# Loads of the gate stage in one order, and each stage's first weights split ahead: a transformer block on one core

## The chip, the cores and the metric

The kernel runs on one core of a Trainium2 chip. The metric is the device time of one execution in microseconds. The core has engines that run side by side, each with its own list of instructions in a fixed order: TensorE (PE in the profile) multiplies matrices, VectorE (DVE) and ScalarE (ACT) work on tiles, GpSimd (POOL) does some of that and issues transfers, SyncE (SP) only issues transfers. An instruction waits for what it needs, and everything behind it on its engine waits with it.

## The reference

One encoder block on 512 tokens of width 2048, in fp32:

```
u   = RMSNorm_pre(h)
[q|k|v|conv_a|conv_b|gate_attn|gate_conv] = u @ W_in
y_A = NeighbourhoodAttention2D(q, k, v; bias) @ W_attn_o        # 8 heads of 128
y_B = ConformerConv(conv_a, conv_b) @ W_conv_o                  # GLU, conv 31, LayerNorm, swish
m   = sigmoid(gate_attn) * y_A + sigmoid(gate_conv) * y_B
h   = h + RMSNorm_post(m @ W_out)
h   = h + RMSNorm_post(SwiGLU(RMSNorm_pre(h)))                  # hidden width 5632
```

## The kernel before

**Products.** Tokens lie along the free axis, so a tile of activations is 128 channels x 512 tokens (a `slot`; u is un0 to un15, 16 tiles). Every fp32 operand is split in two fp32r parts, hi (a cast, on ACT) and lo (operand minus hi, on DVE), and a product is three matmuls: lo x hi, hi x hi, hi x lo. So ahead of each use of weights stand a load (SP's queue, into the pool tag `raw`, 5 buffers of 512 KB), a cast on ACT (names ending in h, or `whi_`) and a subtraction on DVE (`l`, `wlo_`).

**Strassen.** Most of the three large projections run as Winograd's form of Strassen on pairs of output blocks (`strassen`, line 233): seven products instead of eight. Weights come in quarters (tiles q), of which sums are made (s; s1 is made by a load and a second load that adds, `sums`). The activations' side (`operands`) is made once per stage: b11, b2 and the sums t12, t34 (`winograd_t`), each split (`merged`, lines 158 and 159). The products run in the order 11, T2, T1, T3 and so on; one is 8 matmuls with hi (line 265) and 8 with lo (line 267).

**Stages.** After convolution and attention comes the gate stage (lines 555 to 630): the first two of sixteen gate tiles are computed by plain products (tile g, lines 584 to 586), one chunk of u at a time over c = 0 to 7, and while these run, u is loaded back from DRAM (`u_d`), and the Strassen operands of the other tiles are made from it (b, t). The pairs g2, g3 and on follow. Then the gated outputs (`gated`) with the layer norm of the convolution's branch (`layer_norm`, called before tile LN_AT = 8), the output projection, and the FFN: five tiles plain, then pairs f5 to f43 on weights `w_gu`; the result of each pair goes to DRAM (`a_d`, scaled `as_d`). The down projection runs in two stages and a last part (`products_and_operands(n, ...)`, `pairs(n, ...)`, n = 0 and 1, then `half`): first a plain part over four chunks of the FFN (tiles fa, from loads ad; products pd, weights raw_w, whi_wd, wlo_wd, loaded by `weights`), during which the operands of the Strassen pairs are made from rows loaded as da (`prepare(c)`, c = 0 to 7; tiles dt and d), then eight pairs (d_0 to d_14). Results of the first stage are written to `y_d`, later ones added to it by transfers that POOL issues (yf from the plain part, ys from the pairs). The last part has four more chunks (fa40 to fa43, weights wl0 to wl15).

**Order.** A scheduler sets the order of each engine's list when the kernel is built, from program order and its own costs. Instructions marked with `keep_in_program_order` (`load_in_order` for loads) stay in the order in which they are written. Tiles come from pools in turn: a tile of a tag with 5 buffers waits until the tile five before it has been read for the last time. `early(k0)` loads the first three fa of a plain part ahead, `behind_last` splits them behind the last product of the stage before.

Of the kernel before, what the change touches and what calls it, by code (L numbers as in the profile page):

```python
# [25 lines left out]
F32 = mybir.dt.float32  # L26
# [5 lines left out]
P = 128  # L32
# [28 lines left out]
S1_AT = 3  # L61
# [9 lines left out]
def hybrid_block(ctx: ExitStack, tc, xT, vecs, rpb, mask, w_c0, w_qk, w_v, w_gg, w_cg, w_ao, w_co, w_out, w_g0, w_gu, w_dn, outT):  # L71
# [154 lines left out]
    def sums(w1, name):  # L226

        s1 = stp.tile([P, 1024], F32, tag="S1", name=f"{name}s1")
        nc.sync.dma_start(s1, w1[:, :1024])
        nc.gpsimd.dma_start(s1, w1[:, 1024:], accum_op=ALU.add)  # L230
        return s1

    def strassen(w0, w1, op, name, n, s1=None, behind_last=None):
# [8 lines left out]

        def quarter(w, c):
            raw = wp.tile([P, 1024], F32, tag="raw", name=f"{name}q", bufs=5)
            nc.sync.dma_start(raw, w[:, c * 1024 : (c + 1) * 1024])
            return raw
# [11 lines left out]
        def product(ps, w, b, first=False, last=False):  # L258
            hi = wp.tile([P, 1024], F32R, tag="whi", name=f"{name}h")
            nc.scalar.copy(hi, w)  # L260
            lo = wp.tile([P, 1024], F32R, tag="wlo", name=f"{name}l")
            nc.vector.tensor_tensor(out=lo, in0=w, in1=hi.bitcast(F32), op=ALU.subtract)
# [14 lines left out]
        a11, a21, a22, a12 = quarter(w0, 0), quarter(w1, 0), quarter(w1, 1), quarter(w0, 1)  # L277
        product(x, a11, "11", first=True)
# [57 lines left out]

    def rstd_row(acc, n, name):
        out = slot(f"{name}_bc")
        nc.scalar.copy(out, by_column(rstd(acc, n, name), name))
        return out  # L340
# [234 lines left out]
    raw, uf = [], []  # L575
    load_gate(0)
    load_un(0)
    for c in range(HT):
# [37 lines left out]
    for i in range(2, KT):  # L616
        c11, c12, c21, c22 = strassen(w_cg[2 * CT + i], w_cg[2 * CT + KT + i], op, f"g{i}", i + 1, s1 if i == 2 else None)
# [13 lines left out]
    def layer_norm():  # L631
        yc, cv = [], [slot(f"cr{i}") for i in range(CT)]
# [10 lines left out]
        rc = rstd_row(acc, CONV, "rc")  # L643
# [16 lines left out]
        return yc  # L660
# [10 lines left out]
    yg, m = [], []  # L671
    for i in range(KT):
        if i == LN_AT:
            yc = layer_norm()
# [94 lines left out]
    for c in range(HT):  # L769
        hi, lo = wchunk(w_g0[1, c], f"f1_{c}")  # L770
        for k in range(2):
# [64 lines left out]
    acts = []  # L836
    for j in range(5, FT):
        if j == FT - 2:
            behind = early(0)
        c11, c12, c21, c22 = strassen(  # L840
            w_gu[j], w_gu[FT + j], op, f"f{j}", j, behind_last=behind if j == FT - 1 else None
# [26 lines left out]
    def loaded(o, k0):  # L868

        raw = wraw(f"w{k0}_{o}")  # L870
        nc.sync.dma_start(
            raw.rearrange("p (n k) -> p n k", n=2), w_dn[o : o + 2, :, k0 * P : (k0 + DN_P) * P].rearrange("n p k -> p n k")
        )
        return raw

    def weights(o, k0):
        raw = loaded(o, k0)
        return wchunk(raw, f"wd{k0}_{o}", raw=raw)

# [13 lines left out]
    def products_and_operands(n, k0, add):  # L893
# [3 lines left out]
        def load_rows(c):  # L897
            rows.append([slot(f"da{c}_{i}") for i in range(2)])
            for i, t in enumerate(rows[c]):
                nc.gpsimd.dma_start(t, as_d[n * KT + c + i * HT])  # L900

        def prepare(c):
# [3 lines left out]
            u1, u2 = rows[c]  # L906
            b11.append(merged(u1[:, A], f"d11_{c}"))
            b2.append([merged(u2[:, cols], f"d2{c}_{i}") for i, cols in enumerate((A, B))])
            tt = stp.tile([P, 2, NT], F32, tag="S", name=f"dt{c}")
# [235 lines left out]
```

## Time and profile before

| | us |
|---|---|
| median of 3 runs (2541.95 to 2547.01) | 2544.56 |
| profiled execution | 2541.38 |
| its span | 2539.6 |
| PE busy in the span | 2499.8 (98%) |
| DVE busy | 2004.1 (79%) |
| ACT busy | 1194.1 (47%) |
| granted PE clock, mean | 0.995 |

The span runs from the first instruction to the last. A row of the timeline has the start and the duration of an instruction (or of several alike, xN), engine, line, operation, output and inputs, and in brackets the idle time of the engine ahead of it and what ended it. A row of the windows has the stretch in us from the span's start, its length, the busy time of PE, its weight loads, DVE, ACT and POOL with instruction counts, the granted clock, the share of the DMA engines' time and GB/s. A row of the waits names the engine and line that waited, what it waited for, and total, times and longest.

### The profile page before, as it was taken

To read this page: it belongs to the slowest core of one execution; us is meant where nothing else is said; L and a number is where in the kernel's file an instruction comes from. 1 tells how busy PE (TensorE), PEld (TensorE's weight loads), DVE (VectorE), ACT (ScalarE), POOL (GpSimd) and SP (SyncE) were. 2 spreads that over 40 slices of the span, in tenths; PEclk is the share of its full clock that TensorE was granted. 3 is DMA by queue.
4 is the path that set the end of the run, shared out by engine and by line. 5 is a ranking of instruction groups with operands and counts; after the bars stand their busy time and mean duration, and the time that the engine had idled before them with its cause. 6 is when DMAs were issued, how large, how long until landed. Compare 5 with 4: busy or idle time off the path is not lost.

```text
span 2539.6 us, 35631 instructions
## 1 busy us (share of the span) xinstructions
PE 2499.8 (98%) x13415; PEld 2158.5 (85%) x13415; DVE 2004.1 (79%) x2583; ACT 1194.1 (47%) x1822; POOL 477.4 (19%) x521
## 2 busy tenths in 40 slices
PE   9999999989999999999999999999999999999997
PEld 7888888878888888889988888888888888887887
DVE  5999896577776655338798888899998888879886
ACT  5223333355555422225455555555555565456453
POOL 0110222220000011001101111122222124442343
PEclk9999999999999999999999999999999999999998
DMA  6246332476667435327356665666666677889774
GB/s 211 90 146 203 104 101 101 148 246 197 184 183 243 167 126 193 100 99 209 112 157 169 180 180 172 178 202 205 202 199 202 208 255 218 242 218 222 182 223 151
DMA packets 153358, 452.42 MB, mean 178 GB/s; under 512 B 17889, under 2 KB 25185, under 8 KB 153185
## 3 DMA queue, kind: packets, MB, share of 16 engines
q1 hardware_dynamic: 100896, 320.12, 37.5%
q0 software_dynamic: 31616, 94.39, 17.3%
q10 hardware_dynamic: 20672, 35.63, 3.8%
q8 instruction: 105, 1.72, 0.3%
q14 instruction: 69, 0.56, 0.1%
HBM read 381.39 MB, written 61.87 MB: 175 GB/s over the span
## 4 chain that ended last, share of the span: by engine, by line
PE 85%; DVE 8%; issue 3%; DMA 2%; ACT 1%; POOL 1%; ACTq 0%; DVEq 0%; POOLq 0%; SPq 0%
PE f L265 20%; PE f L267 10%; PE d L265 8%; PE g L265 7%; PE d L267 4%; PE g L267 4%; PE qk L186 2%; PE qk L185 2%; PE qk L182 2%; PE po L185 2%; PE po L186 2%; PE po L182 2%; PE py L182 2%; PE py L186 2%; PE py L185 2%
## 5 line engine op out<-in xcount | busy, mean ns | idle before, releaser
L411 DVE SCALAR_TENSOR_TENSOR cv<-z,vec,cv 128x497 f32<-128x497 f32 (+14 forms) x240 | 190.7, 796 | 4.8
L136 DVE TENSOR_TENSOR wlo_wo<-raw_wo,whi_wo 128x1024 fp32r<-128x1024 f32 x36 | 47.4, 1318 | 106.6 <-ACT whi_wo L135 106.3
L801 POOL TENSOR_TENSOR row<-row,asq 128x512 f32<-128x512 f32 x30 | 41.1, 1370 | 413.9 <-ACT asq L800 413.9
L135 ACT CAST whi_wo<-raw_wo 128x1024 fp32r<-128x1024 f32 x36 | 37.9, 1054 | 130.0 <-PE po L185 122.7
L941 POOL TENSOR_TENSOR ys<-ys,row 128x512 f32<-128x512 f32 x32 | 55.7, 1742 | 130.6 <-DVE ys L303 85.4
L135 ACT CAST whi_y<-raw_y 128x1024 fp32r<-128x1024 f32 x32 | 33.5, 1052 | 79.4 <-PE py L185 76.2
L135 ACT CAST whi_qk<-raw_qk 128x1024 fp32r<-128x1024 f32 x32 | 33.7, 1052 | 77.1 <-PE qk L185 56.5
L136 DVE TENSOR_TENSOR wlo_qk<-raw_qk,whi_qk 128x1024 fp32r<-128x1024 f32 x32 | 40.1, 1254 | 32.6 <-ACT whi_qk L135 32.4
L668 DVE TENSOR_TENSOR gg<-py,gg 128x512 f32<-128x512 f32 x32 | 21.8, 689 | 52.7 <-PE py L186 52.7
L828 POOL TENSOR_TENSOR an<-an,row 128x512 f32<-128x512 f32 x32 | 50.7, 1584 | 67.5 <-DMA an<-a_d 42.4
L136 DVE TENSOR_TENSOR wlo_y<-raw_y,whi_y 128x1024 fp32r<-128x1024 f32 x32 | 53.3, 1667 | 10.9 <-ACT whi_y L135 10.0
L323 POOL TENSOR_TENSOR r_r<-r_v,mhalf 128x2 f32<-128x2 f32 (+1 forms) x6 | 7.0, 1171 | 265.8 <-DVE r_v L321 215.4
L182 PE MATMUL py<-ycl,whi_y 128*128 128x512 f32 x128 | 49.8, 389 | 0.0
L185 PE MATMUL py<-ych,whi_y 128*128 128x512 f32 x128 | 49.8, 389 | 0.0
L186 PE MATMUL py<-ych,wlo_y 128*128 128x512 f32 x128 | 49.8, 389 | 0.0
L861 ACT ACTIVATE sg<-sg 128x512 f32<-128x512 f32 x39 | 24.7, 634 | 50.2 <-DVE sg L303 50.2
L492 POOL TENSOR_TENSOR bm<-braw,msk 128x128 f32<-128x128 f32 x56 | 42.4, 791 | 14.8 <-DMA braw<-in_rpb 14.7
L678 POOL TENSOR_TENSOR gg<-gg,gg 128x512 f32<-128x512 f32 x16 | 20.6, 1288 | 112.2 <-ACT whi_y L135 70.7
L419 POOL TENSOR_TENSOR csum<-csum,cv 128x512 f32<-128x512 f32 x7 | 12.7, 1814 | 144.3 <-DVE cv L411 144.3
L164 PE MATMUL f<-b,whi_f 128*128 128x256 f32 x128 | 36.4, 285 | 0.7 <-DVE b L159 0.7
L166 PE MATMUL f<-b,wlo_f 128*128 128x256 f32 x128 | 36.2, 283 | 0.0
L165 PE MATMUL f<-b,whi_f 128*128 128x256 f32 x128 | 36.2, 283 | 0.0
(3196 smaller groups left out, 8752.5 us busy)
## 6 DMA issues: line engine op xcount, KB each, us to landing
raw_wo<-in_w_out SPq DMA_DIRECT2D x36, 512.0 KB, 3.8
raw_qk<-in_w_qk SPq DMA_DIRECT2D x32, 512.0 KB, 3.7
raw_w<-in_w_dn SPq DMA_DIRECT2D x24, 512.0 KB, 5.7
a_d<-sg ACTq DMA_DIRECT2D x44, 256.0 KB, 3.7
raw_v<-in_w_v SPq DMA_DIRECT2D x16, 512.0 KB, 4.3
raw_y<-in_w_ao SPq DMA_DIRECT2D x16, 512.0 KB, 3.8
gg<-g_d SPq DMA_DIRECT2D x32, 256.0 KB, 4.2
raw_y<-in_w_co SPq DMA_DIRECT2D x16, 512.0 KB, 3.6
```

The source lines that it names most:

```text
L135: cast(hi[:, s], raw[:, s])
L136: nc.vector.tensor_tensor(out=lo[:, s], in0=raw[:, s], in1=hi[:, s].bitcast(F32), op=ALU.subtract)
L182: mmul = nc.tensor.matmul(ps, hi[:, s], al, start=first, stop=False)
L185: nc.tensor.matmul(ps, hi[:, s], ah, start=False, stop=False)
L186: nc.tensor.matmul(ps, lo[:, s], ah, start=False, stop=last)
L265: nc.tensor.matmul(ps, hi[:, ws[k]], t, start=first and k == 0, stop=False, skip_group_check=True)
L267: nc.tensor.matmul(ps[:, A], lo[:, ws[k]], t[:, A], start=False, stop=last and k == HT - 1, skip_group_check=True)
L411: nc.vector.scalar_tensor_tensor(out=a[:, to], in0=z[:, fr], scalar=col(C_WDW, i * CW + w), in1=a[:, to], op0=ALU.mult, op1=ALU.add)
L492: nc.gpsimd.tensor_tensor(out=bm[:, o + i - i0], in0=raw[:, :, i * BC : (i + 1) * BC], in1=msk[:, o + i - i0, None, :].broadcast_to([P, RO ...
L801: nc.gpsimd.tensor_tensor(out=row[n], in0=row[n], in1=sq, op=ALU.add)
L828: nc.gpsimd.tensor_tensor(out=t, in0=t, in1=row[k // KT], op=ALU.mult)
L941: tc.keep_in_program_order(nc.gpsimd.tensor_tensor(out=t, in0=t, in1=row[n], op=ALU.mult))
```

## The change

It has five parts.

1. **Gate stage.** The loads of the gate weights (raw_g) join the order that is held, u is loaded one step earlier, and its tiles un4 and un5 of the loop (each of two rows of 512) go to the tag S1 instead of S, which makes two more buffers for u. s1 and the quarters of g2 are loaded in that order too, at c = 5 and from c = 6; s1 of g3 likewise.
2. **First weights.** The first quarter of the first pair of the FFN (f5) and of both down stages is loaded and split (`begun`) ahead of the stage's last preparation; `strassen` takes it as `first`.
3. **Plain parts.** `early`'s function also loads and splits the first weights of the coming plain part (`weights(0, k0)`), or of the last part (`kept(0)`: wl0, wl1).
4. **Layer norm** is cut in three steps, ahead of gated tiles 8, 9 and 10.
5. **Rows for the down stages.** The two rows of a chunk come by one transfer into one tile of the tag `raw`, in place of two into slots; the sums are three DVE operations (one of 512 columns) instead of four.

```diff
@@ strassen's helpers
-    def strassen(w0, w1, op, name, n, s1=None, behind_last=None):
+    def begun(w0, name):
+        a11 = quarter(w0, 0, name)
+        return (a11, *halved_weights(a11, name))
+
+    def strassen(w0, w1, op, name, n, s1=None, behind_last=None, first=None, quarters=None):
...
-        a11, a21, a22, a12 = quarter(w0, 0), quarter(w1, 0), quarter(w1, 1), quarter(w0, 1)
-        product(x, a11, "11", first=True)
+        if quarters:
+            a11, a21, a22, a12 = quarters
+        else:
+            a11 = first[0] if first else quarter(w0, 0, name)
+            a21, a22, a12 = (quarter(*w, name) for w in ((w1, 0), (w1, 1), (w0, 1)))
+        product(x, first[1:] if first else a11, "11", first=True)
@@ the gate stage
     def load_gate(c):
         raw.append(wraw(f"g0_{c}"))
-        nc.sync.dma_start(raw[c], w_gg[c])
+        load_in_order(raw[c], w_gg[c])
     def load_un(c):
-        pool, tag, n = (stp, "S", 2) if c > 1 else (wp, "raw", 5)
+        pool, tag, n = ((wp, "raw", 5), (stp, "S", 2), (stp, "S1", 2), (stp, "S", 2))[c // 2]
...
     load_un(0)
+    load_un(1)
     for c in range(HT):
...
-        if c + 1 < HT:
-            load_un(c + 1)
+        if c + 2 < HT:
+            load_un(c + 2)
         if c == S1_AT:
-            s1 = sums(w_cg[2 * CT + KT + 2], "g2")
+            s1 = sums(w_cg[2 * CT + KT + 2], "g2", load_in_order)
+        if c >= G2_AT:
+            quarters += [
+                quarter(w_cg[2 * CT + KT * n + 2], h, "g2", load_in_order) for n, h in ((0, 0), (1, 0), (1, 1), (0, 1))[
+                    2 * (c - G2_AT) : 2 * (c - G2_AT) + 2
+                ]
+            ]
@@ the FFN
+        if c == HT - 1:
+            first = begun(w_gu[5], "f5")
@@ early
-        return lambda: acts.extend(split(t, f"fa{k0 + k}", pin=True) for k, t in enumerate(raw))
+        def behind_last():
+            acts.extend(split(t, f"fa{k0 + k}", pin=True) for k, t in enumerate(raw))
+            if k0 == DN_3:
+                kept(0)
+            else:
+                w.append(weights(0, k0))
+        return behind_last
@@ products_and_operands
         def load_rows(c):
-            rows.append([slot(f"da{c}_{i}") for i in range(2)])
-            for i, t in enumerate(rows[c]):
-                nc.gpsimd.dma_start(t, as_d[n * KT + c + i * HT])
+            rows.append(wp.tile([P, 2, NT], F32, tag="raw", name=f"da{c}", bufs=5))
+            i = n * KT + c
+            nc.gpsimd.dma_start(rows[c], as_d[i : i + HT + 1 : HT].rearrange("k p t -> p k t"))
...
             if o % 2 == 0:
+                if o == KT - 2:
+                    first = begun(w_dn[0, :, DN_A[n] * P :], f"d{n}_0")
                 prepare(o // 2)
```

What the scheduler makes of it is seen at three places.

PE at the end of the last attention head (s scores, pt transposes, po the head's output, g the gate tiles), before, from the scores' end on:

```order
L513 MATMUL s_3_3985<-qk_1h,qk_0l 128x256
L584 MATMUL g_3_4050<-un0l,whi_g_0_4055 128x512
L585 MATMUL g_3_4050<-un0h,whi_g_0_4055 128x512
L586 MATMUL g_3_4050<-un0h,wlo_g_0_4056 128x512
L585 MATMUL g_1_4048<-un8h,whi_g_0_4055 128x512
L586 MATMUL g_1_4048<-un8h,wlo_g_0_4056 128x512
L584 MATMUL g_2_4049<-un8l,whi_g_0_4055 128x512
L585 MATMUL g_2_4049<-un8h,whi_g_0_4055 128x512
L532 MATMUL pt_0_3997<-ident,sc_0_3956 128x128
```

and now:

```order
L523 MATMUL s_3_3985<-qk_1h,qk_0l 128x256
L542 MATMUL pt_0_3997<-ident,sc_0_3956 128x128
L542 MATMUL pt_0_3997<-ident,sc_1_3967 128x128
L548 MATMUL po_3996<-ptl_0_4001,v_0h 128x256
L549 MATMUL po_3996<-pth_0_4000,v_0h 128x256
L550 MATMUL po_3996<-pth_0_4000,v_0l 128x256
L542 MATMUL pt_3_4007<-ident,sc_2_3978 128x128
```

Between the scores and the transposes stood seven gate products, and more between the transposes and ahead of the scores; now the first gate product follows the head's last po. On ACT the cast whi_g_0, which stood ahead of qk_0h, now follows the head's last cast pth_2; on DVE wlo_g_0 follows ptl_2 in the same way.

POOL at the start of the first down stage (an and as_d are scaled rows of the FFN, ad the loads of fa, da those of the rows), before:

```order
L827 DMA an_18362<-a_d 128x512
L828 TENSOR_TENSOR an_18362<-an_18362,row_10989 128x512
L829 DMA as_d<-an_18362 128x512
L814 DMA ad_18375<-a_d 128x512
L900 DMA da_0_18381<-as_d 128x512
L900 DMA da_1_18382<-as_d 128x512
```

and now:

```order
L944 DMA da_18387<-as_d 128x2x512
L944 DMA da_18389<-as_d 128x2x512
L230 DMA d_2s_19096<-in_w_dn 128x1024
L944 DMA da_18413<-as_d 128x2x512
L857 DMA an_18368<-a_d 128x512
L858 TENSOR_TENSOR an_18368<-an_18368,row_10995 128x512
L944 DMA da_18478<-as_d 128x2x512
L859 DMA as_d<-an_18368 128x512
L844 DMA ad_18381<-a_d 128x512
```

Four loads of rows now stand ahead of ad_18381, which is ad3. The fourth of them takes the buffer of raw_w_2, and so waits for its cast and its subtraction (wlo_wd_2). In the second down stage ad39 stands in the same way behind the da that takes the buffer of raw_w_2 there.

DVE at the start of the second down stage, around the third chunk's sums (dt_20652 before, dt_20616 now; da_..._20467 and da_20447 are the second chunk's rows, dt_20584 and dt_20551 its sums), before:

```order
L159 TENSOR_TENSOR d_1_20530<-dt_20516,d_1_20530 128x256
L204 TENSOR_TENSOR dt_20652<-da_0_20503 128x256
L206 TENSOR_TENSOR dt_20652<-da_1_20504,da_0_20503 128x256
L205 TENSOR_TENSOR dt_20652<-da_1_20504,dt_20652 128x256
L136 TENSOR_TENSOR wlo_wd_8_20689<-raw_w_8_20686,whi_wd_8_20688 128x1024
L159 TENSOR_TENSOR d_1_20575<-da_0_20467,d_1_20575 128x256
L159 TENSOR_TENSOR d_0_20578<-da_1_20468,d_0_20578 128x256
L159 TENSOR_TENSOR d_1_20581<-da_1_20468,d_1_20581 128x256
```

and now:

```order
L159 TENSOR_TENSOR d_3_20499<-dt_20486,d_3_20499 128x256
L159 TENSOR_TENSOR d_1_20542<-da_20447,d_1_20542 128x256
L159 TENSOR_TENSOR d_0_20545<-da_20447,d_0_20545 128x256
L159 TENSOR_TENSOR d_1_20548<-da_20447,d_1_20548 128x256
L159 TENSOR_TENSOR d_0_20555<-dt_20551,d_0_20555 128x256
L159 TENSOR_TENSOR d_2_20558<-dt_20551,d_2_20558 128x256
L159 TENSOR_TENSOR d_1_20561<-dt_20551,d_1_20561 128x256
L955 TENSOR_TENSOR dt_20616<-da_20475 128x512
```

The second chunk's merges, which stood behind the third chunk's sums and behind the split of weight 8, now stand ahead of these sums. On POOL the third, fourth and fifth rows' loads now stand ahead of the first transfer of yf.

More of the change, by code (lines that the diff above doesn't have):

```diff
@@ L258, in product @@
         def product(ps, w, b, first=False, last=False):
[L259 to L262, printed above, removed]
+            hi, lo = w if isinstance(w, tuple) else halved_weights(w, name)
             ws = [slice(k * P, (k + 1) * P) for k in range(HT)]
@@ L631, in layer_norm @@
     def layer_norm():
-        yc, cv = [], [slot(f"cr{i}") for i in range(CT)]
+        cv = [slot(f"cr{i}") for i in range(CT)]
         for i in range(CT):
@@ L833, in early, with loaded, weights, kept @@
         raw = [load_raw(k0 + k) for k in range(EARLY)]
-        return lambda: acts.extend(split(t, f"fa{k0 + k}", pin=True) for k, t in enumerate(raw))
-    acts = []
+        def behind_last():
[5 more added lines that the diff above has]
+        return behind_last
+    def loaded(o, k0):
+        raw = wraw(f"w{k0}_{o}")
+        nc.sync.dma_start(
+            raw.rearrange("p (n k) -> p n k", n=2), w_dn[o : o + 2, :, k0 * P : (k0 + DN_P) * P].rearrange("n p k -> p n k")
+        )
+        return raw
+    def weights(o, k0):
+        raw = loaded(o, k0)
+        return wchunk(raw, f"wd{k0}_{o}", raw=raw)
+    def kept(o):
+        raw = loaded(o, DN_3)
+        w.extend(split(raw[:, i * NT : (i + 1) * NT], f"wl{o + i}") for i in range(2))
+    acts, w = [], []
     for j in range(5, FT):
@@ L840, in hybrid_block @@
         c11, c12, c21, c22 = strassen(
-            w_gu[j], w_gu[FT + j], op, f"f{j}", j, behind_last=behind if j == FT - 1 else None
+            w_gu[j], w_gu[FT + j], op, f"f{j}", j, behind_last=behind if j == FT - 1 else None,
+            first=first if j == 5 else None,
         )
@@ L866, in hybrid_block @@
     left = list(range(FT - DN_A[0] - KT - 2, 2 * KT))
[L868 to L878, printed above, removed]
     def four(ps, hi, lo, cols, pin=False):
@@ L917, in products_and_operands @@
         added()
-        w = [weights(0, k0)]
         for o in range(KT):
@@ L931, in products_and_operands @@
             if o % 2 == 0:
+                if o == KT - 2:
+                    first = begun(w_dn[0, :, DN_A[n] * P :], f"d{n}_0")
                 prepare(o // 2)
         acts.clear()
-        return operands(b11, b2, b_t12, b_t34)
+        w.clear()
+        return first, operands(b11, b2, b_t12, b_t34)
     ys = []
@@ L943, in added, with pairs @@
         ys.clear()
-    def pairs(n, op, k0):
+    def pairs(n, first, op, k0):
         for o in range(0, KT, 2):
@@ L980, in hybrid_block @@
         ha.extend((t[:, 0], t[:, 1]))
-    w, yg, r4 = [], [], []
-    def kept(o):
-        raw = loaded(o, DN_3)
-        w.extend(split(raw[:, i * NT : (i + 1) * NT], f"wl{o + i}") for i in range(2))
+    yg, r4 = [], []
     def half(n, between={}):
@@ L993, in half @@
         if n == 0:
-            for o in range(0, AHEAD, 2):
+            for o in range(2, AHEAD, 2):
                 kept(o)
```

71 lines of the change are left out of this document (43 added, 28 removed).

## The prediction

> **What bounds the kernel now.** I read the page, the waits of PE, then the timeline at each wait.
>
> ```profile
> span 2539.6 us, 35631 instructions
> PE 2499.8 (98%) x13415; PEld 2158.5 (85%) x13415; DVE 2004.1 (79%) x2583; ACT 1194.1 (47%) x1822; POOL 477.4 (19%) x521
> PE g L265 <- DVE b L159: 4.3, 1, 4.3
> PE d L265 <- ACT d_0h L260: 3.5, 2, 2.5
> PE d L267 <- DVE d_0l L262: 2.5, 1, 2.5
> PE g L265 <- ACT g2v L255: 2.2, 1, 2.2
> PE f L265 <- ACT f5h L260: 1.6, 1, 1.6
> PE pl L886 <- DVE wl0l L145: 1.6, 1, 1.6
> PE pl L886 <- ACT wl0h L145: 1.5, 1, 1.5
> PE rc_b L330 <- POOL rc_r L323: 1.1, 1, 1.1
> ```
>
> TensorE (PE) sets the end; 40 us of its span are idle. The waits listed (columns: total, times, longest) make 18.3 us. They are what the change can win; behind two or three of them there is a second price, the clock:
>
> ```profile
> 535.20:538.60 3.40, 3.40 (x12) 3.11 (x13) 3.37 (x8) 2.08 (x5) 0.00 (x0) 0.50 0.00 0
> 2102.00:2105.30 3.30, 3.30 (x8) 2.50 (x8) 3.27 (x4) 1.83 (x2) 1.02 (x2) 0.50 0.37 146
> 529.14 1.75 PE L265 MATMUL g<-b,g2h 128*128 128x512 f32 x7
> 535.17 0.79 PE L265 MATMUL g<-b,g2h 128*128 128x512 f32 x1 [4.28 <-DVE b L159]
> 545.99 2.12 PE L265 MATMUL g<-t,g2h 128*128 128x512 f32 x8 [2.24 <-ACT g2v L255]
> ```
>
> After the waits of 4.28 and 2.5 us the granted clock is 0.50 for 3.4 us, which loses half of that, 1.7 us.
>
> **Gate stage, the gain.** Strassen's first three products (2.79 us each, from 2318.01 to 2320.80 below) would need 8.4 us; from 529.14 to the fourth's start at 545.99 they took 16.85. With u and the weights loaded in one order, DVE's work is no longer behind a late load. A chunk of it is one weight split of 1.22 us (the row 481.70 below) and nine short operations of at most 0.42 (the row 2280.34), 5.0 in all, so eight chunks begun at 492 end by 532, and 192 gate matmuls on PE take longer (below). If so, both waits and the slow clock go: 4.28 + 2.24 + 1.7 = 8.2 us.
>
> **Gate stage, the loss.** In the old order gate products fill PE during the last attention head. The new one (the first order rows above) has none until that head is done, because the split of the first gate weights now stands behind the head's last casts on ACT and DVE.
>
> ```profile
> 480.60:494.70 14.10, 10.19 (x41) 7.25 (x42) 0.00 (x0) 0.00 (x0) 1.00 0.34 109
> 481.70 1.22 DVE L136 TENSOR_TENSOR wlo_g<-raw_g,whi_g 128x1024 fp32r<-128x1024 f32 x1 [4.17 <-ACT whi_g L135]
> 483.59 0.38 PE L511 MATMUL s<-qk_1l,qk_0h 128*128 128x256 f32 x1
> 494.42 0.39 PE L584 MATMUL g<-un9l,whi_g 128*128 128x512 f32 x1
> ```
>
> The first row is a window of the tile g alone: 41 of its matmuls start before 494.70, so 39 before 494.42, where the head's work ends. At 0.227 us each (the chain's row of 182 like ones, below) they are 8.84 us. In the new order the head's own chain is shorter: its first product s starts about 1.2 us earlier, without the split ahead of it, and I let it end at 492.1. The stage's products then start at 492.1 instead of an equivalent 494.42 - 8.84 = 485.6: a loss of 6.5. PE is also nearly idle from 484.3 to 487.7, which by the two slow stretches above should halve the clock once: 1.7 (bounds 0.5 and 3). Together 8.2, and the stage comes out even (bounds -2.5 and +2.5). I take 0.
>
> The Trainium skill, "TensorE: Matmul & The Clock Gate" (What's actually happening), puts it otherwise: the clock halves after a whole idle window of 3.4 us. No such stretch of the head would be wholly idle, and by that rule the loss is 6.5 and the forecast 1.7 lower, which rival (a) takes up. The trace does not agree so far: 2.5 us of idle closed the clock at 2102.
>
> **Layer norm.** Its three steps now lie behind three gated products of 24 matmuls, 5.4 us each, so POOL's power, for which PE waits 1.1 us now, has one of them as cover; the result is used only after five more. If the cover failed, the 1.1 would stay. Gain 1.05, bounds 0.8 and 1.05.
>
> **FFN's first pair.** The split of f5's first quarter is put ahead of the last chunk:
>
> ```profile
> 1240.00:1280.00 40.00, 39.72 (x332) 39.51 (x330) 40.00 (x91) 22.43 (x53) 2.72 (x1) 1.00 0.27 89
> ```
>
> DVE is full there, so the 1.2 us of this split push back the last operands, which the first product needs too. Of the 1.6 waited for f5h I take 0.6 (bounds 0 and 1.2).
>
> **First down stage.**
>
> ```profile
> 2055.96 41.30 PE pd L886 x182
> 2099.12 0.39 PE L886 MATMUL pd<-fa3h,wlo_wd 128*128 128x512 f32 x1
> 2112.55 1.67 PE L265 MATMUL d<-d,d_0h 128*128 128x512 f32 x6 [0.24 <-ACT d_0v L255]
> 2051.49 0.55 POOL L814 DMA_DIRECT2D ad<-a_d  x1
> 2054.07 1.21 DVE L136 TENSOR_TENSOR wlo_wd<-raw_w,whi_wd 128x1024 fp32r<-128x1024 f32 x1
> 2060.59 0.39 PE L886 MATMUL pd<-fa3l,whi_wd 128*128 128x512 f32 x1
> ad<-a_d POOLq DMA_DIRECT2D x4, 256.0 KB, 8.1
> raw_w<-in_w_dn SPq DMA_DIRECT2D x8, 512.0 KB, 6.1
> DMA to landing us min/median/max: 4.2/5.5/9.1
> ```
>
> The plain part ends at 2099.5; the fourth product started at 2112.55. With weights split ahead and no slow clock it would start after three products, a short wait for the second: 2108.9. That is 3.65 gained. But a new wait comes in. The rows da take their buffers from the five that the weights use, and in the new order of POOL (second order rows) the fourth da stands ahead of ad3, the load behind fa3. That da must wait until the split of the second plain weights frees its buffer, 2055.3; ad3, issued at 2051.49 before, goes at 2056.4. ad's loads landed after 5.5 us in the middle of all twelve (the last row, the tile's own) and after 8.1 in this stage (the row of DMA issues, whose last column is the median from issue to landing); the two splits take 1.3. So fa3l is there at 2063.2 to 2065.8. PE wants it 27 matmuls into the stage, at 2061.9 (before: 21). A stall of 1.3 to 3.9; I take 2.2, a little under the middle, since the shorter landing comes from twelve loads and the longer from four. So 1.5 of the 3.65 is left (bounds -1 and 3.65). Behind ad3 on POOL stand only the later da; behind fa3l on DVE the merges of the first chunk, which nothing on PE wants for forty microseconds.
>
> **Second down stage.**
>
> ```profile
> 2311.33 1.22 PE L267 MATMUL d<-d,d_0l 128*128 128x256 f32 x8 [2.49 <-DVE d_0l L262]
> 2313.55 3.68 PE L265 MATMUL d<-d,d_0h 128*128 128x512 f32 x8 [0.99 <-ACT d_0h L260]
> 2318.01 2.00 PE L265 MATMUL d<-d,d_0h 128*128 128x512 f32 x8
> 2320.80 1.55 PE L265 MATMUL d<-d,d_0h 128*128 128x512 f32 x6
> 2280.34 0.42 DVE L206 TENSOR_TENSOR dt<-da,da 128x256 f32<-128x256 f32 x1 [4.50 <-DMA da<-as_d]
> 2280.00:2320.00 40.00, 35.46 (x154) 28.42 (x153) 37.52 (x84) 28.53 (x64) 14.50 (x19) 0.96 1.01 245
> 2266.18 0.39 PE L886 MATMUL pd<-fa39l,whi_wd 128*128 128x512 f32 x1
> 2258.25 1.23 DVE L136 TENSOR_TENSOR wlo_wd<-raw_w,whi_wd 128x1024 fp32r<-128x1024 f32 x1 [0.28 <-ACT whi_wd L135]
> ```
>
> DVE stood 4.50 us for da at 2280.34 and then worked 37.5 of 40 us: it was behind from there to the end. Now da is issued ahead of the y_d adds on POOL, and the first two chunks' merges (2.4 us each) stand ahead of the point of that wait (third order rows). I let the second product start at 2310.9 instead of 2313.55, at full clock: its end moves from 2318.01 to 2313.7, 4.3. Against it stands the same stall as above: ad39 goes behind the da that waits for the split of weight 2, which ends at 2259.5 (row 2258.25); issued at 2260.4, with 5.5 to 8.1 for the landing and 1.3 for the splits, fa39l is there at 2267.2 to 2269.8, and PE wants it at 2266.18. Since DVE sets the end of this part, I charge 0.8 of the 1 to 3.6: gain 3.5, bounds -2 and 5.
>
> **Last stage.**
>
> ```profile
> 2476.09 16.39 DMA raw_w<-in_w_dn
> 2469.96 1.95 DVE L145 TENSOR_TENSOR fa43l<-ad,fa43h 128x512 fp32r<-128x512 f32 x1
> ```
>
> The waits of 1.50 and 1.56 for wl0 go, but nine matmuls on PE wants fa43l, and the chain goes through the last weights' load, with DMA full. That load is issued some 2 us earlier, as its buffer is freed earlier. Gain 1.8, bounds 0.7 and 3.
>
> **Sum.** 0 + 1.05 + 0.6 + 1.5 + 3.5 + 1.8 = 8.45. The profiled execution took 2541.38, its span 2539.6; 2541.38 - 8.45 = 2532.9. The median lies 3.2 above that execution, so I forecast 2536.
>
> **Rivals.**
> (a) The loads of ad land in time and head 7 costs less: the clock stays up there, 1.7 more, and the 2.2 and 0.8 are not lost. 8.45 + 4.7 = 13.15 off: 2531. The clock alone gives 2534, and I give that a third of this case (it is what the Trainium skill's rule of a whole idle window would make here). For it: ad's shortest landing was 4.2. Against it: a load of 512 KB stands ahead of it on its queue.
> (b) No change, the gain is eaten: the head's slow clock lasts two windows (-1.3), the ad stalls take their upper bounds (-1.7 and -2.8), the first of them closes the clock (-1.7), and the last stage gets 0.7 (-1.1). 8.45 - 8.6 = -0.15: 2544.7. For it: in each of these stages something was put ahead in a queue in which others wait. Against it: it needs four upper bounds at once; already two of them, though, bring the time within what can't be told from before.
> (c) Slower: weights and da in one ring of five. Weight 8 may load only when chunk 1 is merged, weight 10 when chunk 2 is, up to 14. A turn of two chunks is a landing, a cast of 1.05 and 3.4 of sums and merges (ten operations of 0.34), against 10.88 us of PE (48 matmuls). At the 6.1 us that these loads took in the first stage (row raw_w) it fits; beyond 6.4 PE pays the rest on every turn. At 9.1, ad's longest, a turn is 13.55: 2.7 too much, three turns a stage, 16 in both. 8.45 - 16 = -7.55: 2552. For it: DMA's share in the window 2280 to 2320 is 1.01, and da's loads are now twice as large. Against it: the weights' loads go through SP's queue, where 6.1 was the middle with ad at 8.1 beside it.
>
> **How the numbers follow.** Forecast 0.44, (a) 0.18, (b) 0.24, (c) 0.14. A measurement of this kernel tells 0.2%, 5.1 us, from no change: faster is below 2539.4, slower above 2549.7. Forecast and (a) are nearly all faster, (b) mostly the same, (c) mostly slower: 0.61, 0.25, 0.14. The range reaches from 2528, the far side of (a), to 2548, which takes in (b) and leaves out most of (c).
>
> **What would show it.** Right: no gate matmul before head 7's po ends, and the gate's first pair without a wait above 0.5 us; a new wait of PE for fa3l and fa39l; rc_r, wl0 and f5 gone from or smaller in the list. Wrong: gate products between the head's transposes; PE waiting for whi_wd or wlo_wd in the middle of a down stage (rival c); a fourth product of either down stage later than the stage's plain end plus 10 us.

## The result, and the profile after

The changed kernel takes 2552.18 us (median of 7 executions, 2546.51 to 2557.58), the kernel before 2544.56 beside it (7 executions): a ratio of 1.0030, 95% interval 1.0017 to 1.0044. It is slower by 0.3%, where 2536 was forecast, which is faster than before. The profiled execution took 2550.05, 8.7 more than the one before. The head of its page, and from the list of what TensorE waits for (total, times, longest, in us):

```profile
span 2548.2 us, 35575 instructions
PE 2504.5 (98%) x13415; PEld 2162.3 (85%) x13415; DVE 2003.3 (79%) x2567; ACT 1194.5 (47%) x1822; POOL 471.1 (18%) x505
PE pd L930 <- DVE fa39l L145: 4.7, 1, 4.7
PE d L276 <- ACT d_0v L269: 3.8, 1, 3.8
PE pd L930 <- DVE fa3l L145: 3.4, 1, 3.4
PE pt L542 <- DVE sc L533: 2.8, 3, 1.4
PE g L276 <- ACT g2h L242: 1.9, 1, 1.9
PE pl L930 <- DVE fa43l L145: 1.8, 1, 1.8
...
PE pl L930 <- DVE wl2l L145: 1.2, 1, 1.2
PE d L276 <- ACT d_0h L242: 1.2, 2, 0.7
```

The waits that the change aimed at are gone or small: b (4.3), d_0h (3.5), d_0l (2.5), f5h (1.6), wl0l and wl0h (1.6 and 1.5) and rc_r (1.1) were in the list of before. Three new ones of 3.4 to 4.7 stand at the top, all in the down stages, and each closes the clock besides: the granted clock is halved behind it. Smaller new ones are pt (2.8, most of it in the last head, which no gate products fill now) and, in the last stage, fa43l and wl2l (1.8 and 1.2), which the list of before doesn't have. Windows of the changed kernel (start and end, length, busy time of PE, PEld, DVE, ACT and POOL, granted clock, DMA share, GB/s); the first five are the 3.4 us ahead of a slow stretch, the last four are slow stretches:

```profile
484.00:487.40 3.40, 0.80 (x6) 0.41 (x4) 3.36 (x12) 2.42 (x7) 0.00 (x0) 1.00 0.00 0
1221.30:1224.70 3.40, 3.40 (x26) 3.17 (x26) 1.20 (x2) 0.45 (x1) 0.95 (x1) 1.00 0.02 5
2064.40:2067.80 3.40, 0.02 (x1) 0.03 (x1) 0.77 (x2) 1.42 (x4) 0.00 (x0) 1.00 0.77 259
2272.60:2276.00 3.40, 0.59 (x3) 0.49 (x4) 1.33 (x4) 1.98 (x6) 0.00 (x0) 1.00 0.66 157
2327.20:2330.60 3.40, 1.16 (x5) 0.99 (x6) 2.74 (x4) 2.03 (x3) 0.00 (x0) 1.00 0.75 205
...
487.40:494.20 6.80, 5.88 (x22) 5.41 (x23) 3.90 (x8) 2.86 (x8) 0.00 (x0) 0.50 0.26 77
1224.70:1228.10 3.40, 3.40 (x10) 2.65 (x9) 0.11 (x1) 0.00 (x0) 1.00 (x1) 0.50 0.43 154
2067.80:2071.20 3.40, 3.40 (x8) 2.72 (x9) 2.71 (x8) 2.67 (x9) 0.71 (x1) 0.50 0.24 30
2276.00:2279.40 3.40, 3.40 (x10) 2.66 (x9) 2.86 (x10) 2.92 (x10) 1.63 (x2) 0.50 0.41 102
```

The fifth slow stretch follows at 2330.6. The kernel before had three, of 3.4 us each (both have one more at the end of the span, from 2525.2 before and 2535.4 now).

**Where the time went.** TensorE has 13,415 matmuls in both kernels. Taking the start of the n-th of them in the one trace and in the other, one sees how far the change is behind at each place (in us; worked out from the two traces, the places on the times of the changed kernel, the forecast beside it as a gain or a loss in the same sign):

| stage | behind at its end | of this stage | forecast |
|---|---|---|---|
| last head and first gate pair (to 556) | 2.3 | +2.2 | 0 |
| later gate pairs | 2.8 | +0.5 | 0 |
| layer norm (to 900) | 1.5 | -1.3 | -1.05 |
| slow stretch at 1224.7 | 3.1 | +1.6 | none |
| f5 (to 1301) | 2.3 | -0.8 | -0.6 |
| first down stage (to 2150) | 4.4 | +2.1 | -1.5 |
| second down stage (to 2336) | 10.3 | +5.9 | -3.5 |
| last stage | 9.1 | -1.2 | -1.8 |

Some 0.4 of it comes back behind the last matmul. Both down stages have the wrong sign, and hold 8.0 of the 9.1. Inside them, by the same comparison: in the first, the wait for fa3l with its slow stretch costs 5.3 and the start of the pairs gains 3.2. In the second, the wait for fa39l with its slow stretch costs 6.6, the start of the pairs gains 6.3 up to the third product, and the wait for d_0v with its slow stretch costs 5.6.

**Why fa3l is late.** GpSimd's queue of the changed kernel at the start of the first down stage, and ScalarE's cast (start, duration, in brackets the idle time ahead and what ended it):

```profile
2052.18 0.72 POOL L944 DMA_DIRECT2D da<-as_d  x1 [6.40 <-DVE f43l L244]
2052.88 0.58 POOL L857 DMA_DIRECT2D an<-a_d  x1
2058.17 1.29 POOL L858 TENSOR_TENSOR an<-an,row 128x512 f32<-128x512 f32 x1 [4.71 <-DMA an<-a_d]
2059.42 0.73 POOL L944 DMA_DIRECT2D da<-as_d  x1
2060.14 0.59 POOL L859 DMA_DIRECT2D as_d<-an  x1
2060.72 0.55 POOL L844 DMA_DIRECT2D ad<-a_d  x1
...
2066.38 0.62 ACT L145 CAST fa3h<-ad 128x512 fp32r<-128x512 f32 x1 [5.56 <-DMA ad<-a_d]
```

and GpSimd's queue of the kernel before at the same place:

```profile
2043.05 0.91 POOL L827 DMA_DIRECT2D an<-a_d  x1
2049.18 1.41 POOL L828 TENSOR_TENSOR an<-an,row 128x512 f32<-128x512 f32 x1 [5.23 <-DMA an<-a_d]
```

The fourth da, on which the forecast looked, waits for nothing when its turn comes at 2059.42. The third one does: it takes a buffer that a quarter of f43's weights holds until f43l is split, and stops GpSimd for 6.40 us. Behind it stands an, whose load goes at 2052.88 instead of 2043.05, and whose landing GpSimd must wait for before it can come to ad3. So ad3 is issued at 2060.72, 9.2 later than before; 2056.4 was forecast. The kernel was 2.3 behind when this stage began, so the queue itself makes 6.9 of the 9.2, and the forecast, worked out on the times of before, missed it by some 2. The landing itself, 5.6 us, is within the forecast's 5.5 to 8.1.

In the second down stage it is the same place in the queue with other neighbours:

```profile
2259.54 0.75 POOL L944 DMA_DIRECT2D da<-as_d  x1 [5.25 <-DVE d_14l L244]
2263.60 2.19 POOL L990 TENSOR_TENSOR ys<-ys,row 128x512 f32<-128x512 f32 x1 [3.31 <-DVE ys L318]
2266.09 0.86 POOL L991 DMA_DIRECT2D y_d<-ys  x1 [0.30 <-POOL ys L990]
2266.72 0.98 POOL L944 DMA_DIRECT2D da<-as_d  x1
2267.45 0.84 POOL L844 DMA_DIRECT2D ad<-a_d  x1
...
2274.02 0.62 ACT L145 CAST fa39h<-ad 128x512 fp32r<-128x512 f32 x1 [5.87 <-DMA ad<-a_d]
```

ad39 stands behind a da that waits 5.25 us for the split of a quarter of the last pair (d_14l) and behind a multiplication of ys that waits 3.31 for VectorE. It goes at 2267.45 instead of the forecast 2260.4; the kernel was 4.4 behind by then, so the queue makes some 2.7 of these 7.1. It lands after 6.5 us.

**Why d_0v is late.** At the end of the second plain part ScalarE copies results into the tiles yf, and then products of the first pair into the tiles d_0v. Both kinds take their buffers from the same three (the tag `quad`), so a copy waits until the transfer of the tile three before has landed. ScalarE, then the matmul that waits:

```profile
2323.91 0.59 ACT L972 COPY yf<-pd 128x512 f32<-128x512 f32 x1 [2.74 <-DMA y_d<-yf]
...
2326.17 0.59 ACT L269 COPY d_0v<-d 128x512 f32<-128x512 f32 x1 [0.72 <-DMA y_d<-yf]
...
2328.80 0.59 ACT L269 COPY d_0v<-d 128x512 f32<-128x512 f32 x1 [1.10 <-DMA y_d<-yf]
...
2329.44 2.81 PE L276 MATMUL d<-d,d_0h 128*128 128x512 f32 x8 [3.78 <-ACT d_0v L269]
```

Experiments below show where this wait belongs: it comes with the shared ring alone and goes with the rows in buffers of their own, but it goes also where the ring stays and da is held in program order. So it takes the ring and the scheduler's order together. The way there I only argue: weights that come late push the plain part's work, and with it the transfers of yf, into its end, where the DMA engines are full (a share of 1.06 from 2310 to 2316). The chain of releases in the trace runs this way: two landings of raw_w (8.48 us from 2290.45, 5.87 from 2300.66), two of yf's transfers (6.97 from 2308.44, 8.20 from 2320.52), then d_0v. How late the weights are is seen in SyncE's queue. In the changed kernel it spreads the last seven loads of plain weights of the first down stage over 44.8 us:

```profile
2046.26 44.76 SPq L877 DMA_DIRECT2D raw_w<-in_w_dn  x7
2094.31 10.02 SPq L236 DMA_DIRECT2D d_0q<-in_w_dn  x4
```

and with the rows da in buffers of their own (an experiment below):

```profile
2046.93 13.80 SPq L877 DMA_DIRECT2D raw_w<-in_w_dn  x5
2075.29 15.51 SPq L236 DMA_DIRECT2D d_0q<-in_w_dn  x4
```

There the last weights are on their way 30 us earlier, and the quarters of the first pair 19; the kernel before has the same 13.80 us, from 2043.95. With one ring of five buffers, each weight waits for the merges of a chunk and each chunk for the split of a weight.

### The profile page after: what moved, and what is told of

It is laid out like the page before. It is cut to its first block, busy times and chain, and to the rows that moved or that the text cites. A ratio compares the mean times of both kernels' runs of the same rounds, so it can differ in the third digit from the quotient of the medians.

```text
span 2548.2 us, 35575 instructions
## 1 busy us (share of the span) xinstructions
PE 2504.5 (98%) x13415; PEld 2162.3 (85%) x13415; DVE 2003.3 (79%) x2567; ACT 1194.5 (47%) x1822; POOL 471.1 (18%) x505
## 4 chain that ended last, share of the span: by engine, by line
PE 81%; DVE 10%; issue 3%; DMA 3%; ACT 1%; POOL 1%; ACTq 0%; DVEq 0%; SPq 0%; POOLq 0%
PE f L276 19%; PE f L278 10%; PE d L276 8%; PE g L276 7%; PE d L278 4%; PE g L278 3%; DVE cv L421 3%; PE qk L186 2%; PE qk L185 2%; PE qk L182 2%; PE po L185 2%; PE po L182 2%; PE py L182 2%; PE po L186 2%; PE py L185 2%
```

## The experiments

Theory A: the down stages lose because the scheduler put the loads of fa3 and fa39 behind loads of da that wait, an accident of the order. Its rival: the shared ring of five costs in whatever order. And for the gate stage: the missing fill of the last head is passed on, or it isn't. Medians in us, each with the kernel before on the same chip, and the ratio of the two with its interval:

| run | median | before | ratio |
|---|---|---|---|
| the change | 2552.2 | 2544.6 | 1.0030 (1.0017 to 1.0044) |
| first gate load free | 2550.1 | 2544.1 | 1.0025 (1.0016 to 1.0034) |
| da held in program order | 2547.3 | 2544.1 | 1.0009 (1.0000 to 1.0018) |
| da in its own buffers | 2539.0 | 2544.1 | 0.9981 (0.9973 to 0.9990) |
| both of the first and third | 2537.2 | 2544.1 | 0.9975 (0.9965 to 0.9984) |
| own buffers, gate stage as before | 2537.9 | 2543.7 | 0.9975 (0.9966 to 0.9984) |
| before, with the shared ring alone | 2557.3 | 2543.7 | 1.0046 (1.0031 to 1.0061) |
| own buffers, no plain weights ahead | 2542.0 | 2543.7 | 0.9987 (0.9977 to 0.9997) |
| the change, da by two loads | 2553.0 | 2543.7 | 1.0031 (1.0022 to 1.0041) |
| own buffers, no first quarters ahead | 2544.5 | 2544.6 | 1.0001 (0.9992 to 1.0010) |
| own buffers, six gate loads free | 2537.9 | 2544.6 | 0.9972 (0.9960 to 0.9985) |
| one load free, weight sum s2 early | 2536.9 | 2545.0 | 0.9971 (0.9960 to 0.9981) |
| six loads free, weight sum s2 early | 2536.4 | 2545.0 | 0.9968 (0.9955 to 0.9980) |

### The first gate load free

```diff
-        load_in_order(raw[c], w_gg[c])
+        (nc.sync.dma_start if c < 1 else load_in_order)(raw[c], w_gg[c])
```

> One word of the change is undone: the load of the first gate weights isn't held in the order, so that g products fill TensorE in the last attention head again, as before the change; the other loads stay held. The profiled execution of the change took 2550.05 us. Theory A (the gate stage's gain was spent on the head's missing fill): the 8.7 us that the change is late at 498 us go, the fourth product of the first pair starts earlier by what the vector engine gains, some 2.3 to 4, and the run takes 2546 to 2548. Rival: the pair's third product waits for the sigmoids of g2h, which come after the landing of g2's sum at 535.2; then the fill buys waiting, the third product still starts at 545 to 546, and the run stays within 1 us of the change (2549 to 2551).

Measured: 2550.05, 2.1 below the change's median (the expectation's figures were set against its profiled execution, 2550.05). TensorE's order in the last head is that of before again, and the 8.7 that the change is behind from 504 us on (495 in the kernel before) are 1.4, as much as that trace is behind ahead of the head. But little of it arrives: the pair now waits for its operands, where the change came too late to wait. Two of its rows:

```profile
536.70 0.79 PE L276 MATMUL g<-b,g2h 128*128 128x512 f32 x1 [3.12 <-DVE b L159]
547.68 2.11 PE L276 MATMUL g<-t,g2h 128*128 128x512 f32 x8 [1.24 <-ACT g2h L242]
```

From the start of the head to the first pair's end the stage is 0.3 behind before, the change 2.2. The time lies in the rival's range; by the traces some 2 of the 8.7 are passed on. With da in its own buffers the same edit gave 1.8 (2539.0 to 2537.2); each of these two differences is inside the intervals, and the sign is the same.

### The rows da held in program order

```diff
-            nc.gpsimd.dma_start(rows[c], as_d[...])
+            tc.keep_in_program_order(nc.gpsimd.dma_start(rows[c], as_d[...]))
```

> The rows da are held in program order, which puts the loads behind fa3 and fa39 back ahead of the fourth da on GpSimd's queue. The ring of five for weights and da, the weights split ahead and the four sums stay. Theory A (the place in the queue costs the down stages): the waits of 3.4 for fa3l and 4.7 for fa39l go with their slow clocks (1.7 each), 8 to 11 us off the change's 2550: 2539 to 2542. Rival (the shared ring costs them): the waits of fa3l and fa39l go, but the end of the second plain part keeps its 3.8 for d_0v with the slow clock behind it, and weights wait for da's buffers in the middle of a plain part: 2 to 6 off, 2544 to 2548.

Measured: 2547.3, 4.9 off the change's median: the rival's range. From its list of waits:

```profile
PE pd L930 <- DVE wlo_wd L136: 8.5, 5, 3.2
PE pd L930 <- DVE fa3l L145: 1.4, 1, 1.4
```

The waits for fa39l and d_0v are gone (the rival had let d_0v stay), and that for fa3l is smaller. In their place TensorE waits five times in the middle of the plain parts for weights, 8.5 in all and 8.2 of it in the second: the waits of the prediction's rival (c), at the place that it named. So the place in the queue is worth some 5; what is left is the ring in this order.

### The rows da in buffers of their own

```diff
-            rows.append(wp.tile([P, 2, NT], F32, tag="raw", name=f"da{c}", bufs=5))
-            i = n * KT + c
-            nc.gpsimd.dma_start(rows[c], as_d[i : i + HT + 1 : HT].rearrange("k p t -> p k t"))
+            rows.append([slot(f"da{c}_{i}") for i in range(2)])
+            for i, t in enumerate(rows[c]):
+                nc.gpsimd.dma_start(t, as_d[n * KT + c + i * HT])
```

with the four sums of before in `prepare`.

> The rows da go back to buffers of their own, each half by a load of its own, with the two halves' sums as before the change; weights split ahead, the gate's order and the layer norm's steps stay as changed. Theory A (the place of the ad loads in the queue is the whole loss of the down stages): like the run with da held in program order, within 2 us. Rival (the ring itself costs): 3 to 6 us faster than that run, with no wait for d_0v at the end of the second plain part: 2536 to 2541.

Measured: 2539.0, 13.1 below the change and 8.3 below the run with da held in order; faster than before. That is the rival's case, and more than the 3 to 6 that it gave against that run. Its list of waits has neither fa3l nor fa39l nor d_0v; for weights it has only this, and the first pairs' old wait in part:

```profile
PE d L276 <- ACT d_0h L242: 3.1, 2, 2.7
PE pd L930 <- DVE wlo_wd L136: 1.1, 1, 1.1
```

### Both: first gate load free, da in buffers of its own

> Both: the first gate load free and the rows da in buffers of their own. If the two losses are apart, the gains of the two runs add: some 3 on top of the run with da's own buffers, 2534 to 2538, 7 to 10 us faster than before the change. If the gate's gain is bound by the landing of g2's sum, nothing on top: within 1 us of that run.

Measured: 2537.2, 0.9975 of before, within the first case's range. It is 1.8 below the run with da's own buffers alone, where some 3 was expected, and this difference is inside the intervals. By the matmuls' starts in its trace the first down stage gains 2.5, the second 3.1 and the last 0.8 over before.

### The shared ring alone, in the kernel before

The change's last part (one ring, one load for both rows, the sums over two blocks) in the kernel before.

> The kernel before the change, with one part of it alone: the rows da share the weights' five buffers, with one load for both halves and the four sums. Theory A (the ring costs by itself): 5 to 13 slower than before, 2549 to 2557, with TensorE waiting for weights or for fa39l. Rival (the ring costs only together with the weights split ahead, which take two of its buffers before the stage starts): within 2.5 of before, 2542 to 2547.

Measured: 2557.3, 13.6 slower than before. That is just above theory A's range (2549 to 2557), and the rival, that the ring costs only together with the weights ahead, is out. The list of waits:

```profile
PE pd L886 <- DVE fa39l L145: 5.8, 1, 5.8
PE pd L886 <- DVE fa3l L145: 3.5, 1, 3.5
PE d L265 <- ACT d_0v L255: 3.4, 1, 3.4
```

The same three as in the change, to within 1.1. They come from this part alone.

### The ring kept, da by two loads

```diff
-            rows.append(wp.tile([P, 2, NT], F32, tag="raw", name=f"da{c}", bufs=5))
-            i = n * KT + c
-            nc.gpsimd.dma_start(rows[c], as_d[i : i + HT + 1 : HT].rearrange("k p t -> p k t"))
+            r = wp.tile([P, 2, NT], F32, tag="raw", name=f"da{c}", bufs=5)
+            rows.append([r[:, 0], r[:, 1]])
+            for i, t in enumerate(rows[c]):
+                nc.gpsimd.dma_start(t, as_d[n * KT + c + i * HT])
```

with the sums of before; r is the tile in the ring (tag raw).

> The change with one piece of its last part undone: the rows da stay in the weights' five buffers, but come by two loads of 256 KB and the sums are taken as before. Theory A (the shared buffers cost): as the change, 2550 to 2554. Rival (the loads of 512 KB, or the sums over two blocks, cost): as the run with da's own buffers, 2538 to 2541.

Measured: 2553.0, as the change. So it is neither the size of the loads nor the sums over two blocks, but the buffers.

### The gate stage as before, da in buffers of its own

The loads of the gate weights, u's buffers and g2's and g3's sums and quarters as before the change.

> The gate stage as before the change (loads not held in one order, u in its old buffers, g2's and g3's sums loaded as before), the rows da in buffers of their own; the layer norm's steps and the weights split ahead stay. The run with da's own buffers alone took 2539.0, and its profile puts its gate stage 1.5 behind before. Theory A (the new order of the gate's loads gains nothing here): 1 to 2 faster than that run, 2537 to 2538, as the run with the first gate load free as well (2537.2). Rival (the held order is worth the 8.2 us of waits that the forecast named, and only the missing fill hid it): 3 or more slower than the run with the first load free, 2540 to 2546.

Measured: 2537.9, 1.2 faster than with the new gate stage and 0.7 slower than with the new one and its first load free; none of these differences is outside the intervals. The new order of the gate's loads brings nothing that can be measured, with or without the fill. The rival (that it is worth the 8.2 of waits) is out.

### Six gate loads free

```diff
-        load_in_order(raw[c], w_gg[c])
+        (nc.sync.dma_start if c < 6 else load_in_order)(raw[c], w_gg[c])
```

on top of da's own buffers.

> As the run with the first gate load free and da's own buffers (2537.2), but the first six loads of the gate's weights are free of the held order. In that run the DMA engines moved nothing from 480 to 490 us, because the weights stood behind u's third load, which waits for memory that the last head's softmax frees at 489. Theory A (the gate's first pair is bound by when the loads land): three loads of 512 KB, some 4.6 us at 340 GB/s, move into that gap, the waits of 4.1 and 2.7 in the pair shrink by 3 to 5, and the run takes 2532 to 2534.5. Rival (the pair is bound by the vector engine's and the scalar engine's own order behind u): within 1 us, 2536 to 2538.5.

Measured: 2537.9, the rival's case. With one load free (the run of both edits above) the DMA engines stand still from 480 to 490 (a share of 0.00), and with six they don't (0.19, 64 GB/s); but VectorE still waits 6 us later on, behind a cast of g2's first quarter:

```profile
526.93 1.23 DVE L244 TENSOR_TENSOR g2l<-g2q,g2h 128x1024 fp32r<-128x1024 f32 x1 [5.99 <-ACT g2h L242]
```

In its trace the gate's fourth product does start 1.9 earlier than with one load free. The median doesn't show it, and one trace against another isn't proof for 1.9.

### No plain weights split ahead

`weights(0, k0)` back inside the plain part, `kept(0)` back at the start of the last part; da in its own buffers.

> As the run with da's own buffers (2539.0), but the plain parts' first weights are split inside their stage again; the first quarters of the first pairs are still split ahead. Theory A (splitting the plain weights ahead is worth the waits that went): the wait for wlo_wd at the start of the plain parts and the 3.1 of wl0 at the last stage come back, 3 to 6 slower, 2542 to 2545. Rival (the first pairs' quarters alone carry the gain): within 1.5, 2538 to 2540.

Measured: 2542.0, 3.0 slower by the medians, at the lower edge of theory A's range. The intervals of the two ratios overlap, and the two profiled executions differ by 0.8 only, so that these 3.0 aren't clear of noise. Of the waits named only those at the last stage come back, for wl0l (1.8) and wl0h (1.5).

The first down stage gains the same 2.4 over before without its weights split ahead.

### No first quarters split ahead

`begun` is called in no stage; da in its own buffers.

> As the run with da's own buffers (2539.0), but the first quarters of the first pairs (of the FFN and of both down stages) are split inside their stage again; the plain weights stay split ahead. Theory A (the quarters carry the gains at the starts of the pairs, 0.9 at f5, 2.4 and 1.3 to 3.1 at the down stages): 3 to 6 slower, 2542 to 2545. Rival (the vector engine is full there, so what is moved ahead comes back behind): within 1.5, 2538 to 2540.5.

Measured: 2544.5, 5.4 slower, theory A's case and outside the intervals; by the medians the first quarters carry more than the plain weights. Its trace has the old wait for f5h (1.9) again, and its first down stage loses 1.4 against before, where that of the run with own buffers gains 2.4.

### The weight sum for the second product early

```diff
                 if o == KT - 2:
                     first = begun(w_dn[0, :, DN_A[n] * P :], f"d{n}_0")
+                    s1 = sums(w_dn[1, :, DN_A[n] * P : (DN_A[n] + KT) * P], f"d{n}_0")
+                    s2 = stp.tile([P, 1024], F32, tag="S", name=f"d{n}_0s2")
+                    nc.vector.tensor_tensor(out=s2, in0=s1, in1=first[0], op=ALU.subtract)
```

and `strassen` takes them; on top of da's own buffers, with one gate load free and with six.

> As the run with the first gate load free and da's own buffers (2537.2); in addition the first pair of each down stage forms its weight sum for the second product (s1 - a11) ahead of the last chunk's sums on the vector engine, instead of behind them. In that run TensorE waits 2.7 for the split of this sum and 1.3 for d_0l at the start of the pairs. Theory A (the vector engine's order at the seam sets the pair's start): 1.5 to 3 faster, 2534 to 2536. Rival (the vector engine is full there, so that the last chunk's operands come later by the 1.2 that the sum takes, and the first or second product waits for those): within 1, 2536 to 2538.5.

> The same with the first six gate loads free (that run took 2537.9, and its profile has the gate's fourth product 1.9 earlier than with one load free). Theory A: 1.5 to 3 faster, 2535 to 2536.5. Rival: within 1, 2537 to 2539.

Measured: 2536.9 and 2536.4, 0.3 and 1.6 less than the runs that they stand on, which the intervals don't tell from nothing. The first lies in its rival's range and the second at the upper end of theory A's, so the question is open. In the first one's list of waits d_0h has shrunk from 3.1, d_0l has grown from 1.3, and d_0v is new:

```profile
PE d L278 <- DVE d_0l L244: 2.0, 2, 1.2
PE d L276 <- ACT d_0v L269: 1.1, 1, 1.1
PE d L276 <- ACT d_0h L242: 0.5, 1, 0.5
```

These two are the lowest medians of the study, 8.1 and 8.7 below before, and both beat the kernel before and the change; which of the versions between 2536 and 2538 is best isn't settled.

## Why the prediction was wrong

**The step that failed is the stall of ad3 and ad39 behind the rows da**, and behind it the price of the ring. The first down stage was put at 3.65 - 2.2 and the second at 4.3 - 0.8; measured are losses of 2.1 and 5.9.

- The prediction saw the right instruction (ad behind da in GpSimd's queue) and the right consequence (a new wait for fa3l and fa39l), and its landing time held: 5.6 and 6.5 within 5.5 to 8.1. It sized the issue by one of the instructions ahead alone, the fourth da. The third da, an with its own landing, and in the second stage a da and the multiplication of ys stand there too, and each may wait. So it put the issue 4.3 and 7.1 too early; less what the kernel was behind by then, some 2 and 2.7. It took 2.2 for the first stall and charged 0.8 for the second; measured are 3.4 (within its 1.3 to 3.9) and 4.7 (beyond its 1 to 3.6).
- It charged no clock for these stalls except in rival (b). Both closed it (2067.8 and 2276.0), 1.7 each. In the first stage this and the stall are nearly the whole error: 5.3 in place of 2.2, against a gain at the start of the pairs of 3.2, forecast as 3.65.
- In the second stage it charged 0.8 of the stall because VectorE sets the end of that part. VectorE is indeed less full in the change (32.14 of the 40 us from 2280, 37.52 before), and the start of the pairs gained 6.3, more than the 4.3 forecast; but the stall and its clock took 6.6 of it. Then the first pair came to wait for d_0v behind the transfers of yf, which the prediction did not follow: 3.8 and a slow stretch, 5.6 together.
- The ring was a rival (c) of 14%, and its time, 2552, is the one measured. That is luck in good part: it was costed as weights that come late on every turn, and in the change TensorE waits only 0.2 for weights. That wait shows up when the order is mended (8.5 in five places). In the change the same shortage of buffers appears as a late ad and a late yf.
- "At the 6.1 us that these loads took in the first stage (row raw_w) it fits" was the argument against (c). It set a turn of 10.55 us (6.1 + 1.05 + 3.4) against TensorE's 10.88, and left out how long a buffer waits in GpSimd's and SyncE's queues between its release and the next load. The run with the ring alone puts the whole of it at 13.6.

**The gains it named were there.** With the rows in their own buffers and the fill in the head, the first down stage gains 2.5 and the second 3.1; the forecast without its stalls was 3.65 and 4.3, so the size was high by some 40%. Layer norm: 1.3 against 1.05, right. f5: 0.8 against 0.6, right. Last stage: 1.2 against 1.8, within its bounds, but not by the waits for wl0: where these 3.1 go, waits of 1.8 for fa43l and 1.2 for wl2l come in their place, so that by the matmuls' starts the stage has gained 0.2 at 2486, and the other 1.0 comes at its last weights (2503).

**The gate stage** was put at 0, within 2.5 either way, and lost 2.2. Its two halves were both off. The loss in the head was put at 8.2 and is 8.7, with the clock closed for two windows of 3.4 us instead of one. The gain was put at 8.2 and is 6.4 (from 8.7 behind to 2.3). It was costed as if no load were late once they are in order, "eight chunks begun at 492 end by 532"; VectorE's last one ends at 540, since u's third load needs memory that the last head's softmax holds until 488, all loads behind it in the held order wait with it, and the DMA engines stand nearly still till then (a share of 0.06 from 470 to 490). And of a fill that was given back some 2 arrived, by one trace against another. So the 8.7 weren't the price of the missing fill; they were mostly time that the stage would have spent waiting.

**The clock in the head.** The row first: PE was busy for 0.80 of the 3.40 us from 484.0, and the clock was 0.50 for the next 6.8. The Trainium skill, "TensorE: Matmul & The Clock Gate" (What's actually happening), has the clock fall after a whole idle window; the trace does not agree, here as little as at 2102 before the change, and the part of rival (a) that rested on it falls.

**What would have shown it wrong** did so: a fourth product later than the plain part's end plus 10 us (13.3 in the second down stage, 2329.44 against the first product's start at 2316.17), and in the run with da held in order, waits for wlo_wd in the middle of a down stage. Of the signs for right, the new waits for fa3l and fa39l came and those for rc_r, wl0 and f5 went, but the gate's first pair kept a wait of 1.9 (g2h).

**Not foreseen and not part of the change:** the slow stretch at 1224.7, 1.6 us, of which the last section tells.

## What to carry to other kernels

When an instruction is moved ahead in a queue, every instruction that it passes inherits its wait, and the price is that of all the waits ahead of the one that matters (here 6.40 us for a buffer and then 4.71 for a landing), not that of the one just ahead: list them all, with what each takes its buffer or its data from. Two streams that share one ring of buffers each wait for the other's consumer; a pace that fits on average says nothing about that, and this kernel lost 13 us by putting a second stream on five buffers that had been enough for the first. Filling an idle stretch of the bound engine is worth only what the stage behind it would not have waited anyway.

## What the runs showed of the hardware

**The slow stretches lie on a grid.** In each of the 14 profiled executions every stretch of half clock begins a whole number of steps of 3.413 us after the end of the first, slow one at the start. In the change: from 487.41 on, 216 steps give 1224.7, 463 give 2067.8, 524 give 2276.0, 540 give 2330.6. The Trainium skill, "TensorE: Matmul & The Clock Gate" (What's actually happening), tells of a free-running window of 3413 ns, which agrees.

**What counts in a window isn't PE's busy time.** The slow stretch at 1224.7 follows 3.4 us in which PE is listed as busy all the time (the second row of the windows at the top). What is special there are 24 matmuls with a single column, in the change:

```profile
1220.73 2.73 PE L328 MATMUL r_s<-ones,h_sq 128*128 128x1 f32 x24
```

The kernel before has the same work, and its clock stays at 1.00:

```profile
1219.26 2.73 PE L313 MATMUL r_s<-ones,h_sq 128*128 128x1 f32 x24
...
1221.00:1224.40 3.40, 3.40 (x20) 2.95 (x21) 1.30 (x2) 0.00 (x0) 1.95 (x1) 1.00 0.09 13
```

Laying these 2.7 us on the grid of each execution gives the share of one window that they fill:

| | share of a window, largest |
|---|---|
| clock closes behind it (9 executions) | 64, 64, 66, 69, 70, 79, 80, 80, 80% |
| clock stays (5 executions) | 53, 54, 57, 57, 59% |

There is no overlap: for this work the boundary lies between 59 and 64% of a window. So the single columns count as idle, or nearly so; listed as busy they would fill the windows. In the other windows of the change behind which the clock closed, PE was busy for 1%, 17%, 24% and 34% (0.02, 0.59, 0.80 and 1.16 of 3.40), so no window has to be wholly idle. Nor are 59 to 64% of idle time a rule for other work: the clock closed behind the first of these two windows of the grid (six gate loads free), with PE busy for 47%, and stayed behind the second (the change), with 45%:

```profile
2466.02:2469.43 3.41, 1.62 (x14) 1.41 (x13) 2.23 (x2) 2.96 (x7) 2.65 (x3) 1.00 1.04 382
...
2269.17:2272.58 3.41, 1.53 (x7) 0.94 (x5) 0.00 (x0) 0.00 (x0) 2.15 (x2) 1.00 0.97 317
```

By PE's listed time the boundary lies near half a window and isn't sharp; what exactly is counted stays open. What follows for a measurement: the same work costs 1.6 us or nothing, by when it comes to lie on the grid, and any change of some 0.2 us ahead of it can decide that. The change lost 1.6 here in its profiled execution, and this says nothing about the change.
